# Strassen's seven block products for the gates of two branches in a two-layer hybrid trunk

## The chip, the cores and the metric

The kernel runs on one core of one Trainium2 chip. The metric is the device time of one execution in microseconds (us), and smaller is better. The engines are named as in the profile: PE (TensorE, the matrix engine; PEld is its loading of the stationary operand), DVE (VectorE), ACT (ScalarE), POOL (GpSimd) and SP (SyncE, which here only issues transfers). SPq and POOLq are the queues of instructions of those two.

## The reference, cut to what matters

One layer is run twice (`DEPTH` is 2), on 256 tokens of 1024 features in float32. `u` is the normalized input, and `proj = u @ w_in` has among its columns three gates of 1024 columns each, one for each branch (pooling, short convolution, differential attention):

```python
u = rms_norm(h, norm_mix_g[i])
proj = u @ w_in[i]
a_in, c_x, c_b, c_c, q, k, v, gates = jnp.split(proj, split_at, axis=-1)
...
g_a, g_b, g_c = jnp.split(jax.nn.sigmoid(gates), N_BRANCHES, axis=-1)
merged = (g_a * (y_a @ w_pool_out[i])
          + g_b * (y_b @ w_conv_out[i])
          + g_c * (y_c @ w_attn_out[i]))
h = h + merged @ w_o[i]
```

So a gate is a product of 256 x 1024 by 1024 x 1024, followed by a sigmoid. The rest of a layer is the inputs of the branches ahead of this, and a squared-ReLU MLP and a gated embedding behind it.

## The kernel before

**Exact float32 products.** PE multiplies float32r operands. Each float32 value is split in two parts, hi and lo, and a product is taken as three: hi by hi, hi by lo, lo by hi. The activations are kept split (`uh`, `ul`). Weights are split as they stream in.

**The weight stream.** All weights pass once through `WeightStream` (L98) in an order fixed by `weight_plan` (L48), in units of 128 x 1024 values (0.5 MB). `load` (L118) fetches two units with one transfer of 1 MB on SP into one of 3 `stage` tiles. `prefetch` (L133) splits a unit: ACT casts `whi` from the stage tile (L144), then DVE subtracts it to get `wlo` (L145). After the second unit of a tile it calls `load` for the tile that follows. `take` (L152), called at the head of every unit's products, splits up to `AHEAD` = 4 units beyond it; the split parts have 5 buffers each.

**Units and side work.** A layer is a list of units (`add`, L360), each a group of matmuls on one unit of weights; `at(u, ...)` (L357) hangs other work behind unit u. One loop at the end issues unit after unit and, behind each, its side work. A scheduler then orders each engine's instructions by that order, with a model of durations, and gives out buffers of each pool as they come free in its model; on the chip every engine works in the order so fixed.

**The merge stage, where the change lies.** `u_b` (L656) is the last unit of the convolution's input. Behind it come 36 units, all by `unit_a` (L261): two k-blocks of 128 x 512 weights by both token tiles, 12 matmuls of 512 columns each. `add_gate` (L751) needs 4 units for 512 columns of one gate, and its `gate` (L732) applies the sigmoid out of PSUM on ACT. `add_proj` (L754) needs 2 units for 512 columns of a branch's projection, and `merge` (L737) multiplies it with the gate and adds (DVE, L740 and L744). The order is: the first branch's two gates, its two projections, then gate and projection by turns for the other two branches. `merge_t` (L746) transposes the sum for the output projection, which follows.

In the first units of that stage there is much side work on DVE: pooling differences (`pool_diff`, L668), the pooling map (`pool_map`, L683), the convolution (`conv`, L705, and `conv_gate`, L716), the attention's norms and outputs (L602 to L625).

Of the kernel before, what the change touches and what calls it, by code (L numbers as in the profile page):

```python
# [8 lines left out]
F32 = mybir.dt.float32  # L9
# [21 lines left out]
UNIT_COLS = {"A": 512, "B": 256, "C": 128, "P": 512}  # L31
# [10 lines left out]
# shape-only constants: identity, 1/count of the first 16 tokens  # L42
# [4 lines left out]

def weight_plan():  # L48
    """Units of 128 x 1024 weights in the order in which they are used.

    ('A', name, layer, k, c): rows of k-blocks k, k+1, columns c..c+511
    ('B', name, layer, k, c): rows of k-blocks k..k+3, columns c..c+255
    ('C', name, layer, k, c): rows of k-blocks k..k+7, columns c..c+127
    ('P', '', layer, 0, 0): the pooling groups' maps, then the layer's transposed embedding
    """
    plan = []
    for i in range(DEPTH):
# [15 lines left out]
        for f in range(2):  # L73
            a("w_in", full, GATE + f * 512)
        for f in range(2):
            a("w_pool_out", half, f * 512)
        for br, nm in ((1, "w_conv_out"), (2, "w_attn_out")):
            for f in range(2):
                a("w_in", full, GATE + br * D + f * 512)
                a(nm, half, f * 512)  # L80
# [16 lines left out]

class WeightStream:  # L98
    """Streams the packed weights and splits each float32 value into the two
    float32r parts that the tensor engine multiplies exactly."""  # L100

    STAGE_BUFS = 3
    AHEAD = 4

    def __init__(self, ctx, tc, w):
        self.nc = tc.nc
        self.w = w
        self.plan = weight_plan()
        self.stage_pool = ctx.enter_context(tc.tile_pool(name="wstage", bufs=self.STAGE_BUFS))
        self.part_pool = ctx.enter_context(tc.tile_pool(name="wpart", bufs=self.AHEAD + 1))  # L110
        self.keep_pool = ctx.enter_context(tc.tile_pool(name="wkeep", bufs=1))
        self.stage = {}
        self.parts = {}
        self.next_dma = 0
        self.next_split = 0
        self.pos = 0

    def load(self, parts=1, between=None):  # L118
        """loads the next two units with one transfer, or with several for an early start;
        between is called after the second of them"""  # L120
        if self.next_dma < len(self.plan):
            t = self.stage_pool.tile([P, 2 * UNIT], F32, tag="stage", name="stage")
            src = self.w[self.next_dma // 2]
            n = 2 * UNIT // parts
            for c in range(0, 2 * UNIT, n):
# [3 lines left out]
            for u in range(2):  # L129
                self.stage[self.next_dma + u] = t[:, u * UNIT:(u + 1) * UNIT]  # L130
            self.next_dma += 2

    def prefetch(self, upto, between=None):  # L133
        while self.next_split < min(len(self.plan), upto):
            u = self.next_split
            src = self.stage.pop(u)
            pool, tag = (self.keep_pool, "keep") if self.plan[u][0] == "P" else (self.part_pool, "w")
# [11 lines left out]
            if u % 2 == 1:  # L149
                self.load()  # L150
# [11 lines left out]
def kernel(  # L162
# [15 lines left out]
    u4 = ctx.enter_context(tc.tile_pool(name="u4", bufs=10))  # L178
# [51 lines left out]
    ws.load()  # L230

# [29 lines left out]
    def unit_a(accs, xh, xl, name, i, k, c, kx, first, last):  # L261
        """accs[t][tok, 512] += x[kx..kx+1].T @ w[k..k+1, c..c+511], both token tiles"""
# [7 lines left out]

    def unit_b(bp, xh, xl, name, i, k, c, kx=None):
        """bp[m][feature, tok] += w[k..k+3, m].T @ x[k..k+3]"""
# [14 lines left out]
    def unit_c(bank, xs, name, i, c):  # L287
        """bank[feature, 0, tok] + bank[feature, 1, tok] = w[:, c..c+127].T @ x"""
# [19 lines left out]
    def transpose_half(xh, xl, src, f, gain, k0=0):  # L308
        """src[t][f] token-major -> feature-major k-blocks 4f..4f+3, times gain, split"""
# [43 lines left out]
    for i in range(DEPTH):  # L353
# [10 lines left out]
        def add_a(accs, xs, name, ks, c, k0=0, kn=KD):  # L364
            """units over k-blocks ks; accs and xs are filled in when they run"""
# [6 lines left out]
        def get(key):  # L372
            if key not in tiles:
                tiles[key] = (bp_tile() if key[0] == "bp" else
# [7 lines left out]
        # -- statistics of the mixer norm  # L382
# [25 lines left out]
        # -- rstd along the free axis, on every partition  # L408
# [12 lines left out]
        # -- q, k: per-(head, half) norm of the scaled rows, then feature-major with gains  # L421
# [26 lines left out]
        # keys of the two halves apart, zeros in the other half's rows  # L448
# [31 lines left out]
        # -- pooling input, conv inputs: feature-major  # L480
# [21 lines left out]
        # -- v  # L502
# [18 lines left out]
        # -- attention scores and exponentials; rows are left scaled by the first half's sum  # L521
# [56 lines left out]
        # -- attention output, per-head norm, feature-major  # L578
# [60 lines left out]
        # -- short convolution inputs  # L639
# [18 lines left out]
        # -- windowed sums by doubling, then the per-group linear map  # L658
# [69 lines left out]
        # -- gated merge of the branches  # L728
        sig = {}
        mg = [[None, None] for _ in range(NT)]  # L730

        def gate(br, f):  # L732
            for t, a in enumerate(tiles.pop(("g", br, f))):
                sig[br, t, f] = t2()
                nc.scalar.activation(out=sig[br, t, f], in_=a, func=AF.Sigmoid, scale=st["rstd"][:, t:t + 1])

        def merge(br, f):  # L737
            for t, a in enumerate(tiles.pop(("p", br, f))):
                sg = sig.pop((br, t, f))
                nc.vector.tensor_mul(out=sg, in0=a, in1=sg)  # L740
                if br == 0:
# [9 lines left out]
        def add_gate(br, f):  # L751
            at(add_a(("g", br, f), xu, "w_in", (0, 2, 4, 6), GATE + br * D + f * 512), gate, br, f)

        def add_proj(br, f, nm, key):  # L754
            u = add_a(("p", br, f), lambda: st[key], nm, (0, 2), f * 512, 0, 4)
            at(u, merge, br, f)
            return u

        for f in range(2):
            add_gate(0, f)  # L760
        for f in range(2):
            add_proj(0, f, "w_pool_out", "ya")
        for br, nm, key in ((1, "w_conv_out", "yb"), (2, "w_attn_out", "yc")):
            for f in range(2):
                add_gate(br, f)
                u = add_proj(br, f, nm, key)
                if br == 2:
                    at(u + 1, merge_t, f)

        # -- output projection, residual, next norm  # L770
# [26 lines left out]
        # -- per-layer embedding projection  # L797
# [10 lines left out]
        # -- MLP: block j of 512 hidden features goes up while block j-1 comes down  # L808
# [69 lines left out]
        # -- gated embedding, residual, next norm or output  # L878
# [20 lines left out]
        # the last columns of the kernel in pieces, so that little is left to do behind the last product  # L899
# [40 lines left out]
def _pack(inp):  # L940
    import numpy as np

    units = []
    for kind, name, i, k, c in weight_plan():
        if kind == "P":
            units.append(np.concatenate([inp["pool_w"][i].transpose(1, 0, 2).reshape(P, 4 * P),
# [49 lines left out]
```

## Time and profile before

| what | value |
|---|---|
| median of 3 runs | 861.3 us (861.02 to 861.81) |
| span of the profiled execution | 859.4 us |
| PE busy | 849.0 us (99%) |
| DVE busy | 582.4 us (68%) |
| ACT busy | 454.8 us (53%) |
| transfers | 158.43 MB, mean 184 GB/s |

The span is the time from the first to the last instruction of one profiled execution. No other time of that execution was taken; its span lies 1.9 us under the median of the runs. A busy time is the time during which an engine worked on at least one instruction; matmuls are pipelined, so that a matmul's own duration is longer than the distance to the next one.

### The profile page before, as it was taken

To read this page: it belongs to the slowest core of one execution; us is meant where nothing else is said; L and a number is where in the kernel's file an instruction comes from. 1 tells how busy PE (TensorE), PEld (TensorE's weight loads), DVE (VectorE), ACT (ScalarE), POOL (GpSimd) and SP (SyncE) were. 2 spreads that over 40 slices of the span, in tenths; PEclk is the share of its full clock that TensorE was granted. 3 is DMA by queue.
4 is the path that set the end of the run, shared out by engine and by line. 5 is a ranking of instruction groups with operands and counts; after the bars stand their busy time and mean duration, and the time that the engine had idled before them with its cause. 6 is when DMAs were issued, how large, how long until landed. Compare 5 with 4: busy or idle time off the path is not lost.

```text
span 859.4 us, 11596 instructions
## 1 busy us (share of the span) xinstructions
PE 849.0 (99%) x4544; PEld 731.3 (85%) x4544; DVE 582.4 (68%) x894; ACT 454.8 (53%) x691; POOL 30.6 (4%) x34
## 2 busy tenths in 40 slices
PE   7999999999999999999999999999999999999998
PEld 5989988888988888888889998888889888888887
DVE  5887886665676666666678877955667666666664
ACT  6664564454654444445664746544446444444462
POOL 2400000000000000000023000000000000000000
PEclk9999999999999999999999999999999999999999
DMA  8754536554545555555455444455554555555531
GB/s 317 289 197 157 186 104 223 185 207 167 193 175 183 188 190 196 196 196 189 158 193 196 168 177 147 148 201 194 194 194 149 196 196 197 191 185 181 184 141 49
DMA packets 24102, 158.43 MB, mean 184 GB/s; under 512 B 2800, under 2 KB 3568, under 8 KB 5488
## 3 DMA queue, kind: packets, MB, share of 16 engines
q1 hardware_dynamic: 23904, 157.66, 51.6%
q8 instruction: 35, 0.57, 0.3%
q14 instruction: 19, 0.16, 0.1%
q10 hardware_dynamic: 144, 0.05, 0.0%
HBM read 156.64 MB, written 1.05 MB: 183 GB/s over the span
## 4 chain that ended last, share of the span: by engine, by line
PE 98%; DMA 1%; SPq 0%; DVE 0%; ACT 0%; issue 0%
PE acc L269 20%; PE acc L268 20%; PE acc L267 20%; PE bp L292 12%; PE bp L293 6%; PE bp L282 4%; PE bp L284 4%; PE bp L280 4%; PE tr L314 1%; PE acc L912 1%; DMA stage<-in_w_dram 1%; PE acc L599 1%; PE tr L445 1%; PE tr L691 0%; PE acc L533 0%; PE acc L534 0%
## 5 line engine op out<-in xcount | busy, mean ns | idle before, releaser
L145 DVE TENSOR_TENSOR wlo<-stage,whi 128x1024 fp32r<-128x1024 f32 (+1 forms) x296 | 359.4, 1216 | 240.9 <-ACT whi L144 239.8
L144 ACT CAST whi<-stage 128x1024 fp32r<-128x1024 f32 (+1 forms) x296 | 308.1, 1045 | 349.4 <-PE acc L269 182.8
L267 PE MATMUL acc<-whi,t 128*128 128x512 f32 x752 | 295.1, 394 | 5.8 <-ACT whi L144 5.8
L268 PE MATMUL acc<-wlo,t 128*128 128x512 f32 x752 | 294.2, 391 | 0.5 <-DVE wlo L145 0.5
L269 PE MATMUL acc<-whi,t 128*128 128x512 f32 x752 | 290.7, 392 | 0.0
L267 PEld LDWEIGHTS acc<-whi,t 128*128 128x128 f32 x752 | 141.5, 188 | 34.8 <-ACT whi L144 6.3
L268 PEld LDWEIGHTS acc<-wlo,t 128*128 128x128 f32 x752 | 141.9, 189 | 29.4 <-DVE wlo L145 1.2
L269 PEld LDWEIGHTS acc<-whi,t 128*128 128x128 f32 x752 | 141.2, 188 | 29.4
L292 PE MATMUL bp<-t,whi 128*128 128x512 f32 x448 | 158.8, 398 | 0.0
L293 PE MATMUL bp<-t,wlo 128*128 128x256 f32 x448 | 125.8, 281 | 0.0
L292 PEld LDWEIGHTS bp<-t,whi 128*128 128x128 f32 x448 | 84.2, 188 | 20.6
L280 PE MATMUL bp<-t,whi 128*128 128x256 f32 x320 | 90.5, 284 | 0.0
L282 PE MATMUL bp<-t,whi 128*128 128x256 f32 x320 | 90.5, 283 | 0.0
L284 PE MATMUL bp<-t,wlo 128*128 128x256 f32 x320 | 90.5, 283 | 0.0
L293 PEld LDWEIGHTS bp<-t,wlo 128*128 128x128 f32 x448 | 84.6, 189 | 0.5
L282 PEld LDWEIGHTS bp<-t,whi 128*128 128x128 f32 x320 | 61.1, 191 | 0.5
L280 PEld LDWEIGHTS bp<-t,whi 128*128 128x128 f32 x320 | 61.0, 191 | 0.5
L284 PEld LDWEIGHTS bp<-t,wlo 128*128 128x128 f32 x320 | 61.2, 191 | 0.0
L304 ACT ACTIVATE t<-tr,par 128x256 fp32r<-128x256 f32 (+1 forms) x56 | 26.2, 502 | 21.0 <-PE tr L445 8.4
L305 DVE SCALAR_TENSOR_TENSOR t<-tr,par,t 128x256 fp32r<-128x256 f32 (+1 forms) x56 | 27.7, 516 | 5.4 <-ACT t L304 5.1
L336 DVE TENSOR_TENSOR t<-t,t 128x256 fp32r<-128x256 f32 (+1 forms) x64 | 28.6, 449 | 0.0
L335 ACT CAST t<-t 128x256 fp32r<-128x256 f32 (+1 forms) x64 | 27.5, 432 | 0.0
(128 smaller groups left out, 516.8 us busy)
## 6 DMA issues: line engine op xcount, KB each, us to landing
stage<-in_w_dram SPq DMA_DIRECT2D x145, 1024.0 KB, 4.8
stage<-in_w_dram SPq DMA_DIRECT2D x4, 256.0 KB, 5.1
stage<-in_w_dram SPq DMA_DIRECT2D x2, 512.0 KB, 9.0
h<-in_x_dram SPq DMA_DIRECT2D x4, 256.0 KB, 10.7
t<-in_xT_dram SPq DMA_DIRECT2D x1, 512.0 KB, 10.1
out_dram<-h SPq DMA_DIRECT2D x2, 256.0 KB, 2.0
out_dram<-h SPq DMA_DIRECT2D x4, 128.0 KB, 1.9
t<-in_xT_dram SPq DMA_DIRECT2D x1, 384.0 KB, 5.6
```

What stands on the lines that cost most here:

```text
L144: self.nc.scalar.copy(out=hi[:, cs], in_=src[:, cs])
L145: self.nc.vector.tensor_sub(out=lo[:, cs], in0=src[:, cs], in1=hi[:, cs].bitcast(F32))
L267: nc.tensor.matmul(accs[t], lhsT=xh[:, kx + j, tk], rhs=wh[:, j, :], start=first and j == 0, stop=False)
L268: nc.tensor.matmul(accs[t], lhsT=xh[:, kx + j, tk], rhs=wl[:, j, :], start=False, stop=False)
L269: nc.tensor.matmul(accs[t], lhsT=xl[:, kx + j, tk], rhs=wh[:, j, :], start=False, stop=last and j == 1)
L280: nc.tensor.matmul(bp[:, m, :], lhsT=wh[:, j, ms], rhs=xh[:, kx + j, :], start=first, stop=False, skip_group_check=True)
L282: nc.tensor.matmul(bp[:, m, :], lhsT=wh[:, j, ms], rhs=xl[:, kx + j, :], start=False, stop=False, skip_group_check=True)
L284: nc.tensor.matmul(bp[:, m, :], lhsT=wl[:, j, ms], rhs=xh[:, kx + j, :], start=False, stop=last, skip_group_check=True)
L292: nc.tensor.matmul(bank, lhsT=wh[:, k, :], rhs=xk, start=k == 0, stop=False, skip_group_check=True)
L293: nc.tensor.matmul(bank[:, 1, :], lhsT=wl[:, k, :], rhs=xk[:, 0, :], start=False, stop=k == KD - 1, skip_group_check=True)
L305: nc.vector.scalar_tensor_tensor(out=lo, in0=src, scalar=g, in1=hi.bitcast(F32), op0=ALU.mult, op1=ALU.subtract)
L336: nc.vector.tensor_sub(out=lo, in0=src, in1=hi.bitcast(F32))
```

## The change

For the first two branches the gate product C = A B is cut in quarters: A by two token halves and two halves of the 1024 features, B by two halves of the features and two halves of the columns. Strassen's scheme needs seven products of quarters instead of eight. A product of quarters, `unit_s`, has two units of 6 matmuls of 512 columns. The gate of the third branch and the projections stay as they were. In each layer the merge stage then has 20 units by `unit_a` and 28 by `unit_s`; the third branch's gate comes first, interleaved with the first branch's products, and the second branch's projections come last.

The sums of quarters of weights are made in two ways. M1 and M3 are made by a DVE operation on a whole stage tile (128 x 2048), in place, with the tile of M2 or M5. M6, M4 and M7 are loaded by SP, and then a second, accumulating transfer on POOL's queue adds the other quarter onto the tile. M2 and M5 are loaded as they are. Sums of the tokens' quarters are made by `token_sums`, in six steps behind units u_b - 4 to u_b + 1, and split again. Four of seven results are copied out of PSUM by ACT (`snap`), and `product_out` combines them on DVE. The stage tiles are 4 instead of 3, the pool `u4` has 9 buffers instead of 10, a fourth load is issued at the start, and the gates and projections that are left take their PSUM banks from the pool `bp`, which the transposes use too.

```diff
+PRODUCTS = ("M2", "M5", "M1", "M3", "M6", "M4", "M7")
...
+def _merge_order():
+    g2 = [("g", 2, f, ks) for f in range(2) for ks in ((0, 2), (4, 6))]
+    s0 = [("S", 0, m) for m in PRODUCTS]
+    s1 = [("S", 1, m) for m in PRODUCTS]
+    p = [[("p", br, f) for f in range(2)] for br in range(3)]
+    order = [g2[0], s0[0], g2[1], s0[1], s0[2], g2[2], s0[3], s0[4], g2[3], s0[5], s0[6]]
+    order += [p[2][0], s1[0], p[2][1], s1[1], s1[2], p[0][0], s1[3], s1[4], p[0][1], s1[5], s1[6]]
+    return order + p[1]
...
+        recipe = {"M2": lambda: ("load", q(0, 0)),
+                  "M5": lambda: ("load", q(1, 1)),
+                  "M1": lambda: ("sub", of["M2"], of["M5"]),
+                  "M3": lambda: ("addto", q(0, 1), of["M5"]),
+                  "M6": lambda: ("sum", q(0, 0), q(0, 1)),
+                  "M4": lambda: ("sum", q(1, 0), q(0, 0)),
+                  "M7": lambda: ("sum", q(1, 0), q(1, 1))}[prod]()
...
-    STAGE_BUFS = 3
+    STAGE_BUFS = 4
...
+        units, (how, *args) = self.transfers[self.next_dma]
+        if how == "sub":
+            t = self.block[args[0]]
+            self.todo[units[0]] = (t, self.block[args[1]], ALU.subtract)
+        else:
             t = self.stage_pool.tile([P, 2 * UNIT], F32, tag="stage", name="stage")
...
+            if how == "sum":
+                self.nc.gpsimd.dma_start(out=t, in_=self.w[self.place[args[1]]], accum_op=ALU.add)
+            elif how == "addto":
+                self.todo[units[0]] = (t, self.block[args[1]], ALU.add)
...
+            if u in self.todo:
+                t, other, op = self.todo.pop(u)
+                self.nc.vector.tensor_tensor(out=t, in0=t, in1=other, op=op)
...
-            if u % 2 == 1:
+            if u in self.last_unit:
                 self.load()
...
-    u4 = ctx.enter_context(tc.tile_pool(name="u4", bufs=10))
+    u4 = ctx.enter_context(tc.tile_pool(name="u4", bufs=9))
...
     ws.load()
+    ws.load()
...
+    def unit_s(bank, xh, xl, prod, i, k, c, first):
+        wh, wl = ws.take("S", prod, i, k, c)
+        for j in range(2):
+            nc.tensor.matmul(bank, lhsT=xh[:, k + j, :], rhs=wh[:, j, :], start=first and k + j == 0, stop=False,
+                             skip_group_check=True)
+            nc.tensor.matmul(bank, lhsT=xh[:, k + j, :], rhs=wl[:, j, :], start=False, stop=False,
+                             skip_group_check=True)
+            nc.tensor.matmul(bank, lhsT=xl[:, k + j, :], rhs=wh[:, j, :], start=False, stop=k + j == 3,
+                             skip_group_check=True)
...
+        def token_sums(step):
...
+            us = st["us"]
+            if step < 2:
+                ks = slice(4 * step, 4 * step + 4)
+                nc.vector.tensor_add(out=us[step], in0=uh_[:, ks, :].bitcast(F32), in1=ul_[:, ks, :].bitcast(F32))
...
+            d = (t4v() if step == 2 else t2().rearrange("p (k t) -> p k t", t=P))
+            nc.vector.tensor_sub(out=d, in0=ops[0], in1=ops[1])
+            split(*parts, d)
...
+        def snap(br, m):
+            s_ = t2()
+            nc.scalar.copy(out=s_, in_=tiles[("s", br, m)])
+            sops["s", br, m] = s_
...
+        def product_out(br, m):
+            s_ = {n: sops.get(("s", br, n)) for n in ("M1", "M2", "M3", "M5")}
+            if m == "M1":
+                nc.vector.tensor_sub(out=s_["M1"], in0=s_["M1"], in1=s_["M2"])
+            elif m == "M3":
+                nc.vector.tensor_sub(out=s_["M3"], in0=s_["M3"], in1=s_["M5"])
+                sigmoid(br, 0, 1, s_["M3"], s_["M3"])
+            elif m == "M6":
+                nc.vector.tensor_add(out=s_["M1"], in0=tiles.pop(("s", br, "M3")), in1=s_["M1"])
+                sigmoid(br, 1, 1, s_["M1"], s_["M1"])
+            elif m == "M4":
+                bank = tiles.pop(("s", br, "M4"))
+                nc.vector.tensor_add(out=s_["M5"], in0=bank, in1=s_["M5"])
+                nc.vector.tensor_add(out=s_["M2"], in0=bank, in1=s_["M2"])
+                sigmoid(br, 1, 0, s_["M2"], s_["M2"])
+            elif m == "M7":
+                nc.vector.tensor_add(out=s_["M5"], in0=tiles.pop(("s", br, "M1")), in1=s_["M5"])
+                sigmoid(br, 0, 0, s_["M5"], s_["M5"])
...
+        for step in range(6):
+            at(u_b - 4 + step, token_sums, step)
```

## Rows read from the trace of the kernel before

**Rows 1.** The page: span, busy times, and the chain's shares by engine.

```profile
span 859.4 us, 11596 instructions
...
PE 849.0 (99%) x4544; PEld 731.3 (85%) x4544; DVE 582.4 (68%) x894; ACT 454.8 (53%) x691; POOL 30.6 (4%) x34
...
PE 98%; DMA 1%; SPq 0%; DVE 0%; ACT 0%; issue 0%
```

**Rows 2.** Waits over the whole span: us in total, times, longest.

```profile
SPq L126 <- DVE wlo L145: 480.8, 93, 11.7
...
ACT whi L144 <- DMA stage<-in_w_dram: 4.9, 8, 1.2
...
POOL rstd L331 <- DVE me L326: 385.7, 3, 300.3
```

**Rows 3.** PE's timeline, first layer's gates: start, us, line (first and thirteenth matmul).

```profile
139.32 0.39 PE L267 MATMUL acc<-whi,t 128*128 128x512 f32 x1
...
142.04 0.39 PE L267 MATMUL acc<-whi,t 128*128 128x512 f32 x1
```

**Rows 4.** Four stretches: length, busy PE, PEld, DVE, ACT, POOL, clock, DMA share, GB/s.

```profile
87.20:98.90 11.70, 11.70 (x82) 10.80 (x81) 10.57 (x28) 5.98 (x10) 0.00 (x0) 1.00 0.43 145
98.90:121.90 23.00, 23.00 (x127) 19.73 (x126) 17.71 (x39) 14.31 (x21) 2.02 (x2) 1.00 0.33 123
121.90:143.60 21.70, 21.70 (x97) 18.00 (x96) 17.05 (x22) 10.98 (x13) 0.00 (x0) 1.00 0.60 207
143.60:200.00 56.40, 56.40 (x254) 46.81 (x253) 33.73 (x37) 26.97 (x31) 0.00 (x0) 1.00 0.54 193
```

**Rows 5.** DVE's timeline where one instruction follows the other.

```profile
127.15 0.68 DVE L336 TENSOR_TENSOR t<-t,t 128x512 fp32r<-128x512 f32 x1
127.75 1.22 DVE L145 TENSOR_TENSOR wlo<-stage,whi 128x1024 fp32r<-128x1024 f32 x1
128.89 0.68 DVE L336 TENSOR_TENSOR t<-t,t 128x512 fp32r<-128x512 f32 x1
```

**Rows 6.** Busy time of one stretch, columns as in rows 4.

```profile
120.00:130.00 10.00, 10.00 (x45) 8.26 (x44) 9.57 (x14) 5.79 (x9) 0.00 (x0) 1.00 0.45 155
```

**Rows 7.** Groups of instructions by form: count, busy us, mean ns, idle before.

```profile
L144 ACT CAST whi<-stage 128x1024 fp32r<-128x1024 f32 x292 | 305.6, 1051 | 347.8 <-PE acc L269 182.8 <-PE bp L292 55.8 <-PE bp L282 50.0
...
L803 ACT COPY t<-bp 128x512 f32<-128x512 f32 x4 | 2.4, 590 | 0.6 <-PE bp L269 0.4
```

**Rows 8.** Weight loads of 1 MB, first layer's merge stage, and their landing.

```profile
L126 SPq DMA_DIRECT2D stage<-in_w_dram x18: 327/328/328, 96.5 to 197.0; - x18
...
DMA to landing us min/median/max: 4.6/4.8/5.5
```

**Rows 9.** Loads of x at the start (line 234), and their landing.

```profile
L234 SPq DMA_DIRECT2D h<-in_x_dram x4: 328/838/1503, 6.1 to 10.7; - x4
...
DMA to landing us min/median/max: 9.3/10.7/11.8
```

**Rows 10.** Busy time of the stretch with most transfers, columns as in rows 4.

```profile
10.00:20.00 10.00, 9.47 (x42) 7.17 (x41) 6.64 (x10) 7.15 (x12) 1.90 (x2) 1.00 1.03 405
```

**Rows 11.** ACT's timeline at the start: the first statistics, and the casts behind.

```profile
19.19 0.62 ACT L300 ACTIVATE t<-h 128x512 f32<-128x512 f32 x1
...
23.53 2.00 ACT L144 CAST whi<-stage 128x1024 fp32r<-128x1024 f32 x2 [0.82 <-DMA stage<-in_w_dram]
```

**Rows 12.** PE's timeline at the start, behind two waits.

```profile
5.80 1.22 PE L267 MATMUL acc<-whi,t 128*128 128x512 f32 x2 [5.80 <-ACT whi L144]
...
7.25 0.63 PE L269 MATMUL acc<-whi,t 128*128 128x512 f32 x1
7.68 0.63 PE L268 MATMUL acc<-wlo,t 128*128 128x512 f32 x1
...
9.81 0.43 PE L268 MATMUL acc<-wlo,t 128*128 128x512 f32 x1
...
14.61 0.50 PE L268 MATMUL acc<-wlo,t 128*128 128x512 f32 x1 [0.53 <-DVE wlo L145]
```

More of the change, by code (lines that the diff above doesn't have):

```diff
@@ L72, in weight_plan @@
             b("w_in", (0, 4), (c, c + 256))
[L73 to L80, printed above, removed]
+        for kind, *what in MERGE_ORDER:
+            if kind == "S":
+                br, prod = what
+                plan.extend(("S", prod, i, k, GATE + br * D) for k in (0, 2))
+            elif kind == "g":
+                br, f, ks = what
+                a("w_in", ks, GATE + br * D + f * 512)
+            else:
+                br, f = what
+                a(PROJ[br], half, f * 512)
         for ks in (low, high):
@@ L95, in weight_plan, with transfer_plan, q, weight_blocks @@
     return plan
+def transfer_plan():
+    out = []
+    plan = weight_plan()
+    u = 0
+    while u < len(plan):
+        if plan[u][0] != "S":
+            n = 2 if u + 1 < len(plan) and plan[u + 1][0] != "S" else 1
+            out.append((tuple(range(u, u + n)), ("load", ("units", *plan[u:u + n]))))
+            u += n
+            continue
+        _, prod, i, _, c = plan[u]
+        def q(h, f):
+            return ("quarter", "w_in", i, 4 * h, c + 512 * f)
+        if prod == "M2":
+            of = {}
+        of[prod] = len(out)
+        recipe = {"M2": lambda: ("load", q(0, 0)),
[5 more added lines that the diff above has]
+                  "M7": lambda: ("sum", q(1, 0), q(1, 1))}[prod]()
+        out.append(((u, u + 1), recipe))
+        u += 2
+    return out
+def weight_blocks():
+    place = {}
+    for _, (_, *args) in transfer_plan():
+        for a in args:
+            if isinstance(a, tuple):
+                place.setdefault(a, len(place))
+    return place
 class WeightStream:
-    STAGE_BUFS = 3
+    STAGE_BUFS = 4
     AHEAD = 4
@@ L108, in __init__ @@
         self.plan = weight_plan()
+        self.transfers = transfer_plan()
+        self.place = weight_blocks()
+        self.last_unit = {units[-1]: n for n, (units, _) in enumerate(self.transfers)}
         self.stage_pool = ctx.enter_context(tc.tile_pool(name="wstage", bufs=self.STAGE_BUFS))
@@ L730, with add_product @@
+        def add_product(br, m):
+            bank = ("s", br, BANK.get(m, m))
+            for k in (0, 2):
+                u = add(lambda k=k: unit_s(get(bank), *sops[OPERAND[m]], m, i, k, GATE + br * D, m not in BANK))
+            if m in ("M2", "M5", "M1", "M3"):
+                at(u, snap, br, m)
+            at(u, product_out, br, m)
         mg = [[None, None] for _ in range(NT)]
         def gate(br, f):
-            for t, a in enumerate(tiles.pop(("g", br, f))):
-                sig[br, t, f] = t2()
-                nc.scalar.activation(out=sig[br, t, f], in_=a, func=AF.Sigmoid, scale=st["rstd"][:, t:t + 1])
+            for t, a in enumerate(tiles.pop(("bpair", "g", br, f))):
+                sigmoid(br, t, f, a, t2())
```

113 lines of the change are left out of this document (77 added, 36 removed).

## Prediction

> **What bounds the kernel now.** I read the page first. PE is busy for 849.0 of 859.4 us, and the chain that ended last is 98% PE [rows 1]. Then the waits: SP's loads wait for DVE to empty a stage tile, but ACT waited for a load only 8 times in the whole run, 4.9 us in all [rows 2]; transfers are hidden. So a matmul less is time gained, as long as nothing else comes up to PE. Next PE's timeline gives the price of one: 12 matmuls of 512 columns lie between starts at 139.32 and 142.04 [rows 3], 0.2267 us each, 2.72 us a unit. Busy time by stretch shows what stands closest behind PE where the change lies: from 87.2 to 200.0 DVE is busy 10.57 + 17.71 + 17.05 + 33.73 = 79.1 of 112.8 us [rows 4]. The second layer repeats it. For a full engine the distance between starts is the price, not the duration: on DVE a split of 1024 columns takes 1.14 us (127.75 to 128.89) and an operation on 512 columns 0.60 (127.15 to 127.75) [rows 5]. In the best stretch DVE is busy 9.57 of 10 us [rows 6].
>
> **What PE gains.** Per branch 8 units of 12 matmuls become 14 of 6: 96 to 84. Two branches and two layers: 48 x 0.2267 = 10.9 us, 1.3%. That is all the change can bring; PE's part of the stretch above falls from 112.8 to 107.4 us in each layer.
>
> **What DVE pays, per layer.**
> - Splits: a unit by `unit_s` feeds half as many matmuls and costs a whole split. 28 units take the place of 16: 12 x 1.14 = 13.7 us.
> - Weight sums M1 and M3, 128 x 2048: no such row. From 512 to 1024 columns the price grows by 0.54, so 1.14 + 2 x 0.54 = 2.22; four make 8.9.
> - `product_out`: one operation of 512 columns for M1, M3, M6 and M7, two for M4: 12 x 0.60 = 7.2.
> - `token_sums`: two sums of 1024 columns, one difference and one split of that size, six operations of 512: 4 x 1.14 + 6 x 0.60 = 8.2.
>
> Together 38.0 us, so DVE wants 79.1 + 38.0 = 117.1 us where PE wants 107.4. DVE becomes the bound here. It can fall behind by the lead of 4 units that it has on entering: 4 x 1.14 = 4.6. That leaves 112.5 us, which without a single gap is what the stretch takes now (112.8); at the best share seen, 0.957, it is 117.6: 4.8 us more per layer, 9.6 in all. The side work of the convolution and the pooling falls into the same first units, where DVE is already busy 17.71 of 23.0 and 10.57 of 11.7 us, so the gaps needed are not there. In the second branch's products, which have merges instead, DVE's 22 splits, sums and outputs (25.1 + 4.4 + 3.6 + 7.2 = 40.3) stand against PE's 40.8 (8 units of 2.72, 14 of 1.36): even.
>
> **ACT.** 12 casts of 1.05, 8 copies out of PSUM of 0.59 [rows 7], about 3 us for the tokens' splits: some 20 us on 58 (5.98 + 14.31 + 10.98 + 26.97 [rows 4]) of 117. Not a bound; the sigmoids keep their number.
>
> **Transfers.** A branch's products need 3 plain loads and 3 pairs: 9 MB where 4 MB were. In a layer's merge stage 28 MB take the place of 18. At 193 GB/s the 16 engines are 0.54 busy [rows 4], so in 117 us the 28 MB ask about 0.7, and 0.86 if an accumulate works twice. The mean fits; the order is the trouble. Of 4 stage tiles M5's is held until M3's sum, M2's until M1's splits. So M6's load can start only when M1's splits are done, SP's later loads queue behind it, and its accumulate waits on POOL for it to land. POOL itself has nothing else then (its longest wait is 300 us) [rows 2]. Between M1's splits and M6's first lie two gate or projection units and M3: 5.44 + 2.72 = 8.2 us at PE's pace. Needed are a load, 4.8 us to landing [rows 8], and an accumulate, which the trace doesn't show. Bounds: below, a plain load's 4.8; above, the 11.8 us of a load in the crowded start [rows 9]. I take 8, nearer to a load that reads both its source and its tile. So M6 is late by 12.8 - 8.2 = 4.6 us (1.4 to 8.4). M4's wait is covered by that one; M7's accumulate queues behind M4's on POOL, and the 5 MB of that group (one plain load, two pairs) need 13 us at the 405 GB/s of the fullest stretch [rows 10], 18 if the two accumulates work twice, and some 2 us to land, against 10.9 + 4.6 = 15.5 us at PE's pace: 0 to 4.6 more. Per branch 1.4 to 13 us, less what else DVE can do meanwhile: in the first branch there are some 16 us of side work, in the second little. DVE's and ACT's order is fixed beforehand, so a late tile also holds work behind it that needs none. I take 2 us for the first branch and 4 for the second: 6 per layer, 12 in all; below, nothing.
>
> The Trainium skill has a rule here (Collectives: The Full Stack, the bandwidth ceiling in Part 3): a reduction by the transfer engines reads two sources for each byte it writes and so comes out at half a copy's rate. By that an accumulate would take about 9.6 us, an estimate from twice the 4.8 above, M6 late by 6.2 instead of 4.6, and the 12 us above would be 16; no run here has shown one yet.
>
> **The rest.** The fourth load at the start goes ahead of x, whose landing took up to 11.8 us [rows 9]; the first statistics run at 19.19, and the casts behind them at 23.53 had waited 0.82 [rows 11]. One MB more at 405 GB/s is 2.6 us: 0 to 2.6, I take 1. `u4` has one buffer less and must hold three more tiles at `u_b`, and the gates now share four `bp` banks with the transposes: 0 to 2 us per layer for both, I take 0.5. In place of a third stage tile the rest of the kernel has a fourth; its loads were not late, so nothing.
>
> **Sum.** 859.4 + 9.6 + 12 + 1 + 1 = 883.0 in the profiled execution; runs lay 1.9 above their span, so 884.9, I say 885. The 10.9 us of PE are in it already, since the stretch is set by DVE.
>
> **The rivals.**
> 1. *DVE bound, accumulates hidden.* If an accumulate takes what a load takes and other work fills the rest, only the 9.6 remain: 859.4 + 9.6 + 1.9 = 871. For it: side work in the first branch, and a scheduler that can put other units first. Against: the tiles held by M2 and M5. Chance 0.20, 862 to 873.
> 2. *Slow accumulates.* At 11.8 us, 13 per branch are lost: 859.4 + 9.6 + 52 + 1.9 = 923. For it: three accumulates queue on one engine. Chance 0.13, from 898 up.
> 3. *PE's clock falls in the waits.* After 5.8 us without work PE's matmuls start 0.43 us apart (7.25 to 7.68), the lower of its levels, 1.2 instead of 2.4 GHz by that distance, until about 9.8; after a wait of 0.53 they don't (14.61) [rows 12]. The stretches of rows 4 show 1.00 throughout. Ten slow matmuls cost 10 x 0.2 = 2 us. If two waits in each of four branches end so, 16 us on top of 885: 901. Chance 0.07. The skill says the same of a PE left idle (TensorE: Matmul & The Clock Gate, Part 1).
> 4. *PE's gain shows.* If DVE's additions fall into its gaps, PE stays the bound and the time is 861.3 - 10.9 = 850.4. It decides at one point: DVE's want per layer in that stretch must stay under PE's 107.4. The sum of counts says 117.1, or 112.5 with the lead; the added 38.0 would have to be 5 to 10 us cheaper than the rows make them. Chance 0.06.
> 5. No change, DVE without any gap at 112.5 against 112.8: 0.04.
>
> **How the numbers follow.** The forecast's own case is 873 to 898, chance 0.50. The range 866 to 913 leaves out rivals 4 and 5 (0.10), the lowest part of rival 1 (about 0.05) and the upper part of rival 2 (about 0.05). A difference under 0.2% can't be told from none here: faster 0.06, same 0.04, slower 0.90.
>
> **What would show it.** Of PE's 4544 matmuls 48 must be gone. Between u_b - 3 and the last merge DVE should be busy over 0.9 of the time in the first branch's products and PE should show idle time before `unit_s`'s first matmuls, put down to DVE's `wlo`; the stretch should grow from 112.8 to some 123 us a layer. Around M6 and M7, ACT's casts or DVE's sums should wait for the stage tile, and accumulates should land 8 us after their issue. If PE still has 98% of the chain, rival 4 was right. The prediction falls if an accumulate lands in 5 us or in over 12, or if the scheduler puts the third branch's units where a tile is late, so that the waits cost nothing.

## The result, and the profile after

The changed kernel takes 921.6 us (median of 4 runs, 919.17 to 922.69) against 861.3 us of the kernel before on the same chip: a ratio of 1.0696, interval 1.0683 to 1.0710. That is 60.3 us more, where 24 were forecast, and 8.6 us above the forecast's range. The profiled execution has a span of 918.9 us, 59.5 more than before.

The page of the kernel after, to be read against [rows 1]: span, busy times, the granted clock in 40 slices, the chain that ended last, and the issues of stage tiles with their median time to landing.

```profile
span 918.9 us, 11716 instructions
...
PE 859.2 (94%) x4496; PEld 733.7 (80%) x4496; DVE 654.8 (71%) x970; ACT 491.4 (53%) x739; POOL 40.6 (4%) x46
...
PEclk9999978989999999999999999879799999999999
...
PE 79%; DMA 9%; DVE 7%; ACT 3%; issue 1%; SPq 0%; POOL 0%; ACTq 0%; POOLq 0%; DVEq 0%
...
stage<-in_w_dram SPq DMA_DIRECT2D x152, 1024.0 KB, 4.8
stage<-in_w_dram POOLq DMA_DIRECT2D x12, 1024.0 KB, 11.1
```

The 48 matmuls are gone (4496 where 4544 were), and still PE is busy for 10.2 us longer than before: matmuls at a lower clock, and small gaps that the busy time swallows. PE's part of the chain fell from 98% to 79%; transfers and DVE have taken 9% and 7% of it. The two dips in the clock line, slices 6 to 9 and 26 to 29, are the merge stages of the two layers. The 12 accumulates land after 11.1 us, the plain loads after 4.8.

The waits that are new, against [rows 2] (engine, line, what it waited for: total, times, longest):

```profile
ACT whi L232 <- DMA stage<-in_w_dram: 54.4, 14, 12.6
...
PE acc L364 <- ACT whi L232: 16.3, 3, 7.4
...
PE bp L356 <- ACT whi L232: 14.7, 2, 8.1
...
PE tr L545 <- DVE t L716: 8.8, 2, 4.4
```

Before, ACT waited 4.9 us for loads in the whole run; now 54.4, once for 12.6. Who these transfers were is told by the view of the accumulates' own line, L210: when they were issued, who waited for them, how long they took.

```profile
L210 POOL DMA_DIRECT2D stage<-in_w_dram x12: 862/862/1056, 117.9 to 649.1; - x12
...
  ACT whi L232: 48.0, 5
...
DMA to landing us min/median/max: 9.4/11.1/12.9
```

Of the 54.4 us, 48.0 stand behind accumulates. Busy time by stretch in the first layer (first row: the stage that was [rows 4], as a whole; columns: stretch, length, then PE, PEld, DVE, ACT and POOL busy, PE's granted clock, DMA share, GB/s):

```profile
87.20:230.00 142.80, 117.36 (x532) 96.07 (x531) 113.62 (x159) 76.56 (x97) 7.47 (x8) 0.90 0.70 219
...
110.00:120.00 10.00, 5.61 (x27) 4.09 (x25) 9.90 (x15) 5.26 (x8) 1.07 (x2) 0.86 0.60 215
120.00:130.00 10.00, 7.92 (x30) 6.83 (x31) 7.65 (x21) 6.17 (x10) 2.96 (x3) 0.63 0.81 206
130.00:140.00 10.00, 9.78 (x48) 7.93 (x47) 10.00 (x15) 7.61 (x11) 0.00 (x0) 1.00 0.99 270
140.00:150.00 10.00, 8.24 (x37) 6.46 (x35) 4.49 (x7) 1.72 (x3) 0.86 (x1) 1.00 0.99 270
150.00:160.00 10.00, 5.90 (x18) 4.72 (x19) 4.63 (x5) 7.00 (x9) 0.00 (x0) 0.66 0.49 177
...
180.00:190.00 10.00, 7.28 (x33) 5.69 (x31) 5.58 (x8) 0.00 (x0) 1.43 (x2) 1.00 1.01 292
190.00:200.00 10.00, 4.46 (x12) 3.09 (x13) 5.23 (x5) 5.09 (x6) 0.86 (x1) 0.66 1.00 236
```

The stretch from 87.2 us on, which held 555 matmuls in 112.8 us before, now holds 532 in 142.8: 30.0 us more in this layer, and the second repeats it. In it PE is idle for 142.8 - 117.4 = 25.4 us, and busy for 10.0 us more than the 107.4 that its matmuls ask at full clock: 25.4 + 10.0 - 5.4 gained = 30.0. Two patterns show. Where DVE is full, PE keeps going at times (130 to 140: DVE 10.00, PE 9.78) and at times doesn't: from 110 to 120, with DVE at 9.90, PE is busy for only 5.61, and then waits 4.41 us at 122.08 for the attention's outputs, which DVE makes (`t L716` in the waits above). From 140 to 150 and from 180 to 190, where the transfer engines are full (0.99 and 1.01) and DVE has nothing left to split, DVE and ACT stand nearly still (4.49 and 1.72; 5.58 and 0.00), and PE runs dry at the end of it.

The timeline around those last two places shows what waited (start, duration, engine, and in brackets the idle time ahead with its releaser):

```profile
140.02 0.86 POOL L210 DMA_DIRECT2D stage<-in_w_dram  x1 [10.74 <-DVE wlo L233]
...
153.00 1.99 ACT L232 CAST whi<-stage 128x1024 fp32r<-128x1024 f32 x2 [10.95 <-DMA stage<-in_w_dram]
154.90 0.68 ACT L874 ACTIVATE t<-bp,rstd 128x512 f32<-128x512 f32 x1
...
154.08 2.36 DVE L233 TENSOR_TENSOR wlo<-stage,whi 128x1024 fp32r<-128x1024 f32 x2 [9.59 <-ACT whi L232]
154.10 0.80 PE L364 MATMUL acc<-whi,t 128*128 128x512 f32 x1 [5.87 <-ACT whi L232]
154.69 0.63 PE L366 MATMUL acc<-wlo,t 128*128 128x512 f32 x1
155.12 0.63 PE L368 MATMUL acc<-whi,t 128*128 128x512 f32 x1
...
192.34 3.88 ACT L232 CAST whi<-stage 128x1024 fp32r<-128x1024 f32 x4 [12.59 <-DMA stage<-in_w_dram]
...
195.34 1.22 PE L356 MATMUL bp<-whi,t 128*128 128x512 f32 x2 [8.05 <-ACT whi L232]
...
211.61 0.50 PE L364 MATMUL acc<-whi,t 128*128 128x512 f32 x1 [3.07 <-ACT whi L232]
```

An accumulate issued at 140.02 lets ACT go at 153.00. ACT stands at the head of its own list with the cast of the late tile; behind it wait sigmoids of results that PE had done before it ran dry (L874, 154.90), and DVE's work behind those. PE idles 5.87 us, and its next matmuls start 0.43 us apart, as in [rows 12], where 0.23 is full clock. At 192.34 it is the same, and PE's first matmuls after it belong to a plain unit (`bp`, L356), whose weights need no sum at all: it is a unit of `unit_a`, and its cast stood behind those of the late tile.

The chain of that second place (start, duration, what):

```profile
165.29 2.20 DVE stage L224
...
169.83 4.55 DVE wlo L233 x4
174.39 4.75 DMA stage<-in_w_dram
179.70 12.56 DMA stage<-in_w_dram
192.57 0.73 issue
193.29 2.93 ACT whi L232 x3
```

This is the main mechanism in six rows: a late DVE (a weight sum, then four splits without a gap) gives a stage tile back at 174.39; only then can the first quarter be loaded, 4.75 us; only after that can the second be added, 12.56 us; with the issue between them 18 us from the tile's release (174.39) to ACT's cast (192.34).

### The profile page after: what moved, and what is told of

Same layout as the page of the kernel before. It is cut to its first block, busy times and chain, and to the rows that moved or that the text cites. A ratio compares the mean times of both kernels' runs of the same rounds, so it can differ in the third digit from the quotient of the medians.

```text
span 918.9 us, 11716 instructions
## 1 busy us (share of the span) xinstructions
PE 859.2 (94%) x4496; PEld 733.7 (80%) x4496; DVE 654.8 (71%) x970; ACT 491.4 (53%) x739; POOL 40.6 (4%) x46
## 4 chain that ended last, share of the span: by engine, by line
PE 79%; DMA 9%; DVE 7%; ACT 3%; issue 1%; SPq 0%; POOL 0%; ACTq 0%; POOLq 0%; DVEq 0%
PE acc L356 12%; PE acc L358 12%; PE acc L357 12%; PE bp L392 11%; DMA stage<-in_w_dram 9%; PE bp L393 6%; PE bp L384 4%; PE bp L382 4%; PE bp L380 4%; DVE wlo L233 4%; PE bp L357 2%; PE bp L358 2%; PE bp L356 2%; ACT whi L232 2%; PE acc L364 1%
## 5 line engine op out<-in xcount | busy, mean ns | idle before, releaser
L233 DVE TENSOR_TENSOR wlo<-stage,whi 128x1024 fp32r<-128x1024 f32 (+1 forms) x320 | 384.7, 1214 | 221.2 <-ACT whi L232 219.9
L232 ACT CAST whi<-stage 128x1024 fp32r<-128x1024 f32 (+1 forms) x320 | 330.7, 1045 | 343.6 <-PE acc L358 106.7
L356 PE MATMUL acc<-whi,t 128*128 128x512 f32 x464 | 182.5, 396 | 7.8 <-ACT whi L232 6.2
L357 PE MATMUL acc<-wlo,t 128*128 128x512 f32 x464 | 182.2, 393 | 0.0
L358 PE MATMUL acc<-whi,t 128*128 128x512 f32 x464 | 179.1, 394 | 0.0
L356 PEld LDWEIGHTS acc<-whi,t 128*128 128x128 f32 x464 | 87.7, 189 | 26.8 <-ACT whi L232 6.6
L357 PEld LDWEIGHTS acc<-wlo,t 128*128 128x128 f32 x464 | 87.7, 189 | 17.7 <-DVE wlo L233 0.2
L358 PEld LDWEIGHTS acc<-whi,t 128*128 128x128 f32 x464 | 87.2, 189 | 18.1
L356 PE MATMUL bp<-whi,t 128*128 128x512 f32 x160 | 60.0, 402 | 14.7 <-ACT whi L232 14.7
L364 PE MATMUL acc<-whi,t 128*128 128x512 f32 x112 | 49.8, 444 | 17.2 <-ACT whi L232 16.3
L358 PE MATMUL bp<-whi,t 128*128 128x512 f32 x160 | 62.3, 390 | 0.0
L357 PE MATMUL bp<-wlo,t 128*128 128x512 f32 x160 | 62.3, 389 | 0.0
## 6 DMA issues: line engine op xcount, KB each, us to landing
stage<-in_w_dram POOLq DMA_DIRECT2D x12, 1024.0 KB, 11.1
t<-in_xT_dram SPq DMA_DIRECT2D x1, 512.0 KB, 10.4
```

The source lines that it names most:

```text
L232: self.nc.scalar.copy(out=hi[:, cs], in_=src[:, cs])
L233: self.nc.vector.tensor_sub(out=lo[:, cs], in0=src[:, cs], in1=hi[:, cs].bitcast(F32))
L356: nc.tensor.matmul(accs[t], lhsT=xh[:, kx + j, tk], rhs=wh[:, j, :], start=first and j == 0, stop=False)
L357: nc.tensor.matmul(accs[t], lhsT=xh[:, kx + j, tk], rhs=wl[:, j, :], start=False, stop=False)
L358: nc.tensor.matmul(accs[t], lhsT=xl[:, kx + j, tk], rhs=wh[:, j, :], start=False, stop=last and j == 1)
L364: nc.tensor.matmul(bank, lhsT=xh[:, k + j, :], rhs=wh[:, j, :], start=first and k + j == 0, stop=False, skip_group_check=True)
```

## The experiments

Theory A is that the accumulates' waits are the loss; theory B that DVE's added work is. The first four runs take away one, the other, both, or only the adding. One caution holds for most of them: an edit changes the program that the scheduler orders. In experiment 2 every engine has its instructions in the order of the kernel after; in experiments 1, 3, 4, 5 and 6 ACT's, DVE's and PE's lists are in another order than there, and so they are in 8, 10 and 12 against the runs that they are compared with. These differences hold the new order too, and no run separates it.

**1. Without the second transfers.**

```diff
-            if how == "sum":
-                self.nc.gpsimd.dma_start(out=t, in_=self.w[self.place[args[1]]], accum_op=ALU.add)
```

> Leaves out the second, accumulating transfer of M6, M4 and M7 (12 in all); these three use one quarter of the weights. Everything else stays. Theory A (the accumulates, landing 11.1 us after issue, cost most of the loss; by the waits of the first layer some 19 us of PE idle and the slow clock behind them): about 871 us (866 to 882), clock back near 1.0. Theory B (DVE's added work is most of it, the tiles are late because DVE frees them late): 895 us or more.

Measured: 873.7 us, 1.0150 of the time before (1.0120 to 1.0179). All of DVE's added work is in it, and the loss is 12.4 us; the second transfers, with the order that they bring, are worth the other 47.9.

**2. The second transfers without the adding.** The same issue on POOL without `accum_op`: it overwrites the tile instead.

```diff
-                self.nc.gpsimd.dma_start(out=t, in_=self.w[self.place[args[1]]], accum_op=ALU.add)
+                self.nc.gpsimd.dma_start(out=t, in_=self.w[self.place[args[1]]])
```

> The second transfer stays on POOL's queue, of the same size into the same tile and behind the same wait, but overwrites instead of adding (the sums of M6, M4 and M7 are left out). If the adding is what is slow: it lands 5 to 7 us after issue instead of 11, and the time is 872 to 890. If the order (load, wait, second transfer, 9 MB where 4 were) is what costs: it stays over 905.

Measured: 893.5 us, 1.0380 (1.0331 to 1.0429). Each engine has its instructions in the same order as after, so the difference to 921.6 is the adding alone: 28.1 us. The other 893.5 - 873.7 = 19.8 us lie between this run and experiment 1: a second transfer that must follow the first, whatever it does, and the order. The view of its line:

```profile
  ACT whi L232: 15.0, 4
...
DMA to landing us min/median/max: 5.0/6.2/10.0
```

6.2 us to landing instead of 11.1, and 15.0 us of ACT's waits instead of 48.0.

**3. Without DVE's weight sums** of M1 and M3 (eight operations in the run).

```diff
-            if u in self.todo:
-                t, other, op = self.todo.pop(u)
-                self.nc.vector.tensor_tensor(out=t, in0=t, in1=other, op=op)
```

> Leaves out the two weight sums per branch on DVE (M1 and M3 then use one quarter of the weights), 8 operations of about 2.2 us. Theory A: they save what DVE is over in the first branch only, 4 to 6 us a layer, so 909 to 915, and the waits for accumulates stay. Theory B: all 18 us come back and a part of the clock, 895 to 903.

Measured: 891.6 us, 1.0358 (1.0328 to 1.0388): 30.0 us less than after, for eight operations that take 18.2 us together. Taking DVE's work away gains more than the work itself; theory A alone doesn't give this. ACT still waits for accumulates in this run, 45.6 us where it was 48.0, but in ten waits of at most 7.2 us instead of five of up to 12.6; PE's idle time (span less busy time) falls from 59.7 to 34.0 us.

**4. Neither** (both edits).

> Leaves out both the second transfers and the DVE sums. Theory A, with DVE still the bound at 117.1 - 8.9 us of wanted work per layer: 860 to 866, near the kernel before. If the two losses feed each other (late DVE, late loads), it lies below what the two single ones add up to. If PE were free of all waits, 850.

Measured: 863.4 us, 1.0025 (1.0014 to 1.0036). Alone the two edits gain 47.9 and 30.0, 77.9 together; in one kernel they gain 58.2. So they are not two separate losses: 77.9 is more than the whole loss, and more than the 71.2 us down to a kernel that keeps all of PE's saving (921.6 - 850.4). Without accumulates DVE's sums cost 873.7 - 863.4 = 10.3, with them 30.0. And even without any weight sum, PE's 48 saved matmuls don't show in the time. They do show in PE's busy time, 840.3 us, 8.7 less than before; but PE is idle for 19.6 us where it was 10.4.

**5. Five stage tiles** instead of four (paid for by one buffer less of `wlo` and of `u2`), so that a load can start earlier.

```diff
-    STAGE_BUFS = 4
+    STAGE_BUFS = 5
```

> The change with 5 stage tiles instead of 4 (paid with one lo buffer and one small tile less; the whole computation). If the waits come from tiles that M2 and M5 hold, so that M6, M4 and M7 start to load too late: 885 to 905. If the accumulates are slow by what runs beside them, or if DVE's lateness moves everything: 912 or more.

Measured: 903.9 us, 1.0500 (1.0469 to 1.0530): 17.6 less than after. The wait for a free tile looks to be part of the loss (the buffers given up for it and the new order are in the number too); the accumulates still land after 11.9 us.

**6. Thin sums:** DVE's sums on 8 of 2048 columns, the tiles held as before.

```diff
-                self.nc.vector.tensor_tensor(out=t, in0=t, in1=other, op=op)
+                self.nc.vector.tensor_tensor(out=t[:, 0:8], in0=t[:, 0:8], in1=other[:, 0:8], op=op)
```

> The DVE sums of M1 and M3 cover only 8 of 2048 columns (the rest of these sums is left out): DVE's 2.2 us each are gone, but M5's tile is still held until M3's sum and every wait stays. If DVE's time made up the 30 us that the run without sums gave back: 890 to 896. If it was the tile that came free sooner: 905 to 915.

Measured: 897.4 us, 1.0423 (1.0384 to 1.0462). Of experiment 3's 30.0 us, 24.2 come back without the sums' time on DVE, and the last 5.8 only when M2's and M5's tiles aren't held for them either; both runs have an order of their own.

**7. An accumulate by itself, first try:** the kernel before, with 12 transfers into a scratch tile, meant for the MLP; accumulating in the first layer, plain in the second.

```diff
+            if i == 0:
+                nc.gpsimd.dma_start(out=scratch, in_=w[n + 20], accum_op=ALU.add)
+            else:
+                nc.gpsimd.dma_start(out=scratch, in_=w[n + 20])
```

> The kernel before, with six accumulates of 1 MB into a tile that nobody reads in the first layer's MLP, and six plain loads of 1 MB from POOL's queue in the second layer's, beside the normal weight loads at about half of the engines. If an accumulate is slow in itself: 10 us or more to landing. If it lost to the loads beside it in the merge stage: 6 to 8 us. The plain ones 5 to 6. The time stays within 2 us of 861.3.

Measured: 881.1 us in one run. As a measurement beside quiet engines it failed: nothing tied the transfers to the MLP, and the scheduler put them at 25 to 141 us. The time shows something else. The accumulates landed after 12.2 us (median). Two waits of that trace, and POOL's timeline ahead of them:

```profile
DVE ors L614 <- POOL ors L331: 13.1, 2, 11.0
...
PE acc L267 <- DVE t L616: 12.6, 1, 12.6
...
123.36 0.53 POOL L865 DMA_DIRECT2D scratch<-in_w_dram  x1 [8.05 <-DMA scratch<-in_w_dram]
123.90 1.04 POOL L331 TENSOR_TENSOR ors<-oms,mhalf 128x4 f32<-128x4 f32 x1
```

A small operation on POOL (`ors`) stood in POOL's list behind a transfer that waited for the one before it, and PE lost 12.6 us at one blow, in a kernel whose data hang on none of them. These were plain transfers (L865, the second layer's, which the scheduler had put at 104 to 141 us): it is the waiting on POOL's queue that cost this, not the adding.

**8. POOL takes half the splits** of Strassen's units, in the kernel of experiment 4: can the gain of PE be had, if DVE is relieved?

```diff
-                self.nc.vector.tensor_sub(out=lo[:, cs], in0=src[:, cs], in1=hi[:, cs].bitcast(F32))
+                eng = self.nc.gpsimd if self.plan[u][0] == "S" and self.plan[u][3] == 2 else self.nc.vector
+                eng.tensor_sub(out=lo[:, cs], in0=src[:, cs], in1=hi[:, cs].bitcast(F32))
```

> As e4 (neither second transfers nor DVE sums), and the subtraction for the second unit half of each product's units goes to POOL, 28 of 56. If DVE's work is what eats the 10.9 us that PE saves: DVE is about 16 us a layer lighter and the time is 850 to 857. If POOL is too slow for it, or slows DVE's reads: 862 or more.

Measured: 871.4 us, 1.0121 (1.0080 to 1.0162), 8 us more than experiment 4. Groups by line (busy, mean ns of one):

```profile
L229 DVE TENSOR_TENSOR wlo<-stage,whi 128x1024 fp32r<-128x1024 f32 (+1 forms) x292 | 363.8, 1251 | 194.1 <-ACT whi L227 192.6
...
L229 POOL TENSOR_TENSOR wlo<-stage,whi 128x1024 fp32r<-128x1024 f32 x28 | 74.4, 2657 | 195.8 <-ACT whi L227 189.5 <-DVE t L809 6.2
...
L710 DVE TENSOR_TENSOR ors<-ors,rz 128x4 f32<-128x4 f32 x4 | 9.4, 2340 | 0.6 <-POOL ors L427 0.6
```

A split on POOL takes 2.66 us, over twice DVE's 1.22, and DVE's own splits grew from a mean of 1215 ns in experiment 4 to 1251. DVE gave away 28 operations, some 28 x 1.215 = 34.0 us, and is busy for 643.8 us where it was 637.8: what it kept takes 40.0 us longer. The mean of the splits hides how. Some DVE operations last until POOL's subtraction ends, however small they are; the last row is one on 128 x 4 values, four of them at 2.34 us each, where experiment 4 has 0.16:

```profile
L709 DVE TENSOR_TENSOR ors<-ors,rz 128x4 f32<-128x4 f32 x4 | 0.6, 157 | 0.0
...
113.89 2.39 POOL L229 TENSOR_TENSOR wlo<-stage,whi 128x1024 fp32r<-128x1024 f32 x1
113.95 2.34 DVE L710 TENSOR_TENSOR ors<-ors,rz 128x4 f32<-128x4 f32 x1 [0.30 <-POOL ors L427]
```

(The first row is experiment 4's, the other two experiment 8's timeline.) DVE's splits have a median of 1.22 us as before, and the longest takes 3.33.

**9. One branch, spaced.** Strassen for the second branch only, behind the side work of the first units, its products mixed with plain units so that more lies between an accumulate's issue and its use. The tokens' sums come six units later.

```diff
-    order = [g2[0], s0[0], g2[1], s0[1], s0[2], g2[2], s0[3], s0[4], g2[3], s0[5], s0[6]]
-    order += [p[2][0], s1[0], p[2][1], s1[1], s1[2], p[0][0], s1[3], s1[4], p[0][1], s1[5], s1[6]]
+    order = g2 + [g0[0], m["M2"], g0[1], m["M5"], m["M1"], g0[2], m["M3"], p[2][0], m["M6"],
+                  g0[3], p[2][1], m["M4"], p[0][0], m["M7"], p[0][1]]
```

> Seven products for the second branch alone, the whole computation: behind the pooling and convolution side work, alternating with plain units of 2.72 us, and with a projection pair more ahead of M6, M4 and M7 each. PE saves 12 matmuls a layer, 5.4 us in all. If the loss is DVE's saturated first units and accumulates without time to land: DVE wants about 33 us where PE wants 41, the accumulates have some 14 us each, and the time is 856 to 860. If accumulates hurt whatever the spacing (engines full, tiles held): 863 to 880.

Measured: 888.3 us, 1.0321 (1.0299 to 1.0343). Missed, and above the rival too. Two steps of its chain:

```profile
142.82 4.71 DMA stage<-in_w_dram
148.13 13.24 DMA stage<-in_w_dram
```

The same pair as after, load and then accumulate, 18.6 us long. Why the greater distance doesn't cover it was not isolated; the plain units put between the products use stage tiles and queues too.

**10. One branch, without second transfers** (experiments 9 and 1 together).

> As e9 without the second transfers (M6, M4 and M7 use one quarter; six transfers gone). What PE saves must show if DVE was the only other bound: 855.5 to 858. Its distance to e9 is what the accumulates still cost.

Measured: 863.0 us, 1.0023 (1.0013 to 1.0033). Missed. Half the accumulates cost 25.2 us here (888.3 - 863.0), about half of the 47.9. And the 5.4 us that 24 matmuls fewer should give are not there; PE is busy for 846.9 us, 2.1 less than before. Its windows, where the branch lies:

```profile
130.00:140.00 10.00, 9.38 (x40) 7.14 (x39) 10.00 (x16) 7.01 (x8) 0.00 (x0) 1.00 0.22 91
140.00:150.00 10.00, 9.50 (x42) 7.46 (x42) 10.00 (x12) 6.58 (x9) 0.00 (x0) 1.00 0.90 320
150.00:160.00 10.00, 10.00 (x46) 8.29 (x45) 10.00 (x12) 6.62 (x8) 0.00 (x0) 1.00 0.87 329
```

DVE is full for 30 us, and PE has 40, 42 and 46 matmuls in these windows, where the kernel before has 45, 46 and 46 in the same column.

**11. An accumulate by itself, second try:** as 7, each transfer tied by a one-column copy on ACT to the MLP block that it should run beside.

```diff
+            nc.scalar.copy(out=scratch[:, 0:1], in_=st["s", n - 1][0][:, 0, 0:1].bitcast(F32))
```

> The kernel before with six accumulates of 1 MB in the first layer's MLP and six plain loads from POOL's queue in the second layer's, one per block of the MLP, tied to the block's own data so that they can't go earlier. An accumulate beside a half-full set of engines: 6 to 8 us to landing if it lost to its neighbours in the merge stage, 10 or more if it is slow by itself. Plain: 5 to 6. Time within 2 us of 861.3, since nothing waits for them.

Measured: 862.2 us in one run, so nothing is lost there. Accumulates land after 8.6 us (median, 8.5 to 11.0), the same transfers without adding after 7.6 (5.2 to 8.2). Windows, without and with one accumulate (the first two), with one plain transfer, with none, with one (the last three):

```profile
300.00:312.00 12.00, 12.00 (x63) 10.22 (x62) 5.88 (x7) 5.51 (x8) 0.00 (x0) 1.00 0.60 197
312.00:324.00 12.00, 12.00 (x60) 10.09 (x59) 8.98 (x15) 6.18 (x12) 0.86 (x1) 1.00 0.96 283
713.00:725.00 12.00, 12.00 (x61) 10.08 (x61) 8.56 (x15) 6.81 (x13) 0.53 (x1) 1.00 0.73 275
725.00:736.00 11.00, 11.00 (x59) 9.41 (x58) 5.71 (x7) 4.86 (x7) 0.00 (x0) 1.00 0.55 193
736.00:747.00 11.00, 11.00 (x56) 9.21 (x55) 7.97 (x15) 6.04 (x11) 0.53 (x1) 1.00 0.78 286
```

The DMA share (last column but one) rises by 0.36 of 12 us with one accumulate, 4.3 us of all 16 engines, and by 0.18 of 12 to 0.23 of 11 with one plain transfer, 2.2 to 2.5 us. GB/s rise about alike (86; 82 and 93). Against the same windows of the kernel before (0.54; 0.51 and 0.53) it is 5.0 us with an accumulate, and 2.6 and 2.8 with a plain transfer. Either way adding about doubles the engines' time for the same megabyte.

The Trainium skill (Collectives: The Full Stack, the bandwidth ceiling in Part 3) puts a reduction in a ring of cores at half a copy's rate because it reads two sources. This trace agrees in the factor, 4.3 against 2.2 to 2.5 us of the engines' time; what is read it doesn't show. The estimate of 9.6 us to landing in the prediction lies between the 8.6 beside half-empty engines and the 11.1 in the merge stage.

**12. One branch, spaced, five tiles** (experiments 9 and 5).

> As e9 with 5 stage tiles (one lo buffer and one small tile less). If e9 still waits for tiles held by M2 and M5: 2 to 10 us under e9. If e9 hides them already: within 1 us of it.

Measured: 884.1 us, 1.0270 (1.0249 to 1.0290): 4.2 less than with four tiles. The accumulates land after 11.4 us.

No version of these is faster than the kernel before.

## Why the direction was right and the time too low

**PE's saving** was right in count: 48 matmuls less, and nothing of it seen in the time, since PE no longer sets the end of the stage.

**DVE's cost** held. Forecast were 38.0 us of added work per layer; busy time rose by (654.8 - 582.4) / 2 = 36.2. A weight sum was put at 2.22 us by extrapolation; the chain has 2.20. Without accumulates the kernel took 873.7 us (experiment 1), where the rival with DVE as the bound and hidden accumulates gave 871. The place was another than the prediction's sign, which was PE idle for `wlo` ahead of `unit_s`: after, that is 3.0 us in all, while the attention's outputs, held up on DVE, cost PE 6.5 us per layer (4.41, 1.39 and 0.68 in the first), and 13.3 us in experiment 1, most of PE's new waits there. The start, put at 1 us, cost 0.35: a matmul that is 0.35 us later at 88 us than before. No run isolates the 0.5 us per layer put down for `u4` and `bp`.

**The step that failed is the accumulates' wait**, "2 us for the first branch and 4 for the second: 6 per layer, 12 in all". By experiment 1 it is 47.9 us in all. The sign and the place were right (M5's and M2's held tiles, ACT's cast waiting for the stage tile, the fixed order behind it); the size was off fourfold. By the trace alone, PE's idle time behind late tiles is 28.0 us: 5.87 and 8.05 in the first layer, 7.40 and 6.64 in the second. The reasons:
- *Landing.* Taken were 8 us, between 4.8 and 11.8; the median is 11.1, the longest 12.9. Experiments 2 and 11 show why: an accumulate asks twice the engines' time of a plain transfer, and in this stage the engines are 0.99 to 1.01 busy with it. The text saw the crowding ("the mean fits; the order is the trouble"), and priced the landing outside of it. Making it plain gives 28.1 us back.
- *Serial pairs.* The load and the accumulate of one tile follow each other, 4.75 and 12.56 us, and the load starts only when a tile is free. The forecast counted this in full for M6 alone; it let M4 be covered by it, and gave M7 0 to 4.6 us. In the first branch of this trace it is the third accumulate (140.02), M7's, that PE waits for. Even with a plain second transfer 19.8 us are lost, and a fifth tile gives 17.6 of the 60.3 back.
- *A late DVE makes late tiles.* The prediction added the DVE term and the wait term as if they were apart. They feed each other: a tile is free when DVE has split it, so a DVE that is behind moves a chain of 18 us, and during that chain DVE itself stands still (9.59 us at 154.08), which it then has to make up. That the two losses lengthen each other is what experiments 1, 3 and 4 say: the same eight sums are worth 10.3 us without accumulates and 30.0 with. The way is read from the chain and not shown apart: without the sums ACT waits for accumulates nearly as long in all (45.6 us), only in shorter pieces, of which PE notices less.
- *The order fixed beforehand.* The prediction named it, and then took side work as cover. ACT's sigmoids and a plain unit's cast stood behind the late tile's cast instead. It also costs where no tile is late: the 3.07 us at 211.61 are a cast that stood behind a sigmoid, which waited 5.7 us for DVE; experiment 2, whose transfers land after 6.2 us, has the same wait.
- *PE's clock*, the third rival. After the waits at 154.10 and 196.76 PE's matmuls start 0.43 us apart for 8 and 4 distances, at the lower of its two levels (1.2 GHz by that distance); in the whole stage of the first layer there are 25 such distances, 25 x 0.2 = 5.0 us, so some 10 in both layers, of the rival's 16. Its chance of 0.07 was too low. It is no case of its own: in the first layer it stands behind each of PE's four waits of 3.07 to 8.05 us.

**The second rival**, 923 us with landings at 11.8, all but met the time. By the runs its terms come near too: 52 us of waits against experiment 1's 47.9, and 9.6 for DVE against the 12.4 that are left. By the trace its mechanism is only a part: PE idles for 28.0 us behind late tiles, not 52. The slow clock behind the waits (some 10), the waits for the attention's outputs (6.5 per layer) and those at M7, behind ACT's and DVE's order (3.8 and 2.3), make up most of the rest; of these the rival had only DVE's part, in its 9.6. That its sum fits so well is in part luck.

**What stays open.** Experiments 4 and 10 have no accumulates, and 4 no sums either, and neither is faster than before, though experiment 4 asks DVE for 8.9 us per layer less than experiment 1, and experiment 10 has one branch instead of two. In experiment 4 part of the answer is seen: 4.9 us of PE's idle time are waits for the attention's outputs on DVE, 2.4 in each layer. That DVE, at 10.00 of 10 us, has no slack left for PE to gain from is what the windows of experiment 10 suggest, but a run with a truly faster DVE was not had: experiment 8 meant to be one and made DVE slower. Open too is how much of each difference is the scheduler's new order; only experiment 2's 28.1 us are free of it.

## What to carry to other kernels

Price a scheme that saves matmuls by what each matmul's operand costs to make: here a unit of weights fed half the matmuls for a whole split, and 1.3% of PE's time was bought with 36 us of DVE's per layer. Price an accumulating transfer as a chain (tile free, load, then an add at twice the engines' time, in the crowding of that very stage), and where a busy engine frees the tile, price the engine's delay and the transfer's wait together: the same sums cost 10.3 us alone and 30.0 with the accumulates. Before an in-order engine is given an instruction that waits for a transfer, read what stands behind it.

## What was not expected of the hardware

- An accumulate of 1 MB takes 4.3 us of all 16 engines against 2.2 to 2.5 for a plain transfer from the same queue, and lands after 8.6 us beside half-empty engines, 11.1 beside full ones; the same transfers without adding took 7.6 and 6.2.
- A subtraction of 128 x 1024 values takes POOL 2.66 us and DVE 1.22, and while POOL does one, some of DVE's operations last until it ends: 2.34 us for 128 x 4 values that took 0.16. In all 28 of them, 74.4 us on POOL, went with 40.0 us more on DVE for the work that it kept. The Trainium skill (SBUF — State Buffer, "Who interferes with whom") says that a DVE operation with two inputs in SBUF contends with POOL's reads; the trace agrees: `ors` has two such inputs.
- A transfer that waits on POOL's queue, adding or not, holds whatever small operation stands behind it: 11.0 us for DVE, which needed `ors`, and 12.6 for PE in experiment 7.
